# A two-block network in one launch: in its linear-attention layer the weights' low parts move to VectorE, the state is carried to the middle of the next block, the head norm's weights are applied after the transposition, and pools start elsewhere

## The chip, the cores and the metric

The kernel runs on one core of one Trainium2 chip, in one launch. The metric is the device time of one execution in microseconds. Before the change the median of three timed runs is 2821.83 us (2821.72 to 2823.71). Nothing is batched: 512 tokens of width 1024 go through the whole network once, and everything is computed in float32 accuracy.

## The reference, cut to what matters

The network is a chain of nine stages: an "even" layer (recurrence), an "odd" layer (gated linear attention), a feed-forward, a stick-breaking attention, two feed-forwards with shared keys and values between them, a sparse attention and a last feed-forward. The change touches the odd layer; of it, per head (4 heads, keys 128 wide, values 256 wide) and per direction (forward and backward):

```
z = lr @ w_gate + b_gate;  g = log_sigmoid(z) / 16
bcum = cumsum(g in a block);  btot = its last
q_in = q * exp(bcum);  k_in = k * exp(-bcum);  k_st = k * exp(btot - bcum)
o_intra = (mask * (q_in @ k_in.T)) @ v
o_inter = q_in @ state;   state = exp(btot) * state + k_st.T @ v
o = rmsnorm(o_f + o_b, head_norm_g);   y = (o * silu(r)) @ w_out
x = x + rmsnorm(y, norm_post)
```

The kernel uses blocks of 128 tokens, so there are four blocks and, per head and direction, three state updates.

## The kernel before, in words

Every product in full accuracy is three matmuls. A float32 operand is split into a high part, rounded to the chip's fast float32 format, and a low part, the rest; `mm3` (lines 88 to 92) issues high x high, high x low and low x high into one PSUM tile. So each 128x2048 slab of weights that arrives by DMA (`wload`, lines 75 to 86, tile `ws`) costs two ScalarE copies of 128x1024 (`wh`, line 84) and two subtractions of 128x1024 (`wl`, line 85). The subtraction is on VectorE, or on GpSimd where the caller passes `eng=nc.gpsimd`. There are two buffers each of `ws`, `wh` and `wl`; SyncE issues all DMAs, and the next slab's DMA waits until the subtraction has read `ws`.

The odd layer (`odd`, lines 601 to 864) starts with `begin` (query and key products of heads 0 and 1 while the stage before still finishes), and then runs a loop of 48 steps, 12 for each head, written in lines 832 to 859. The loop calls, step by step: `scaled` and `scores` (query and key scaled by the decay, block products `A`, transposed keys `KT`), `state` (line 685: the product `U` of keys and values of a block, the new state `S`, and its split into `Sh`, high and low), `decay` of the next head (line 627: the gate's logarithm, a scan over 512 tokens, exponentials), `outputs` (line 730: products into PSUM tile `o`, squares for the norm, statistics `st`), and at a head's end `gated` (line 752: `o` times norm times gate, transposed by TensorE into `ot`, split into `oh` and `ol`). Between them the list `dense` hands out the dense products of other heads: `queries`, `values`, `gate` and `out`, with a due step for each piece. In the whole layer 13 slabs (heads 1 to 3 of values, heads 2 and 3 of queries, all gates, three output slabs, and the first slab of the feed-forward behind) have their low part on GpSimd. A scheduler then sets each engine's order from these calls; each engine runs its instructions in that fixed order and waits on semaphores.

In `decay`, the minimum of line 636 is on VectorE and the subtraction of line 637 on GpSimd. In `state`, `S` is carried as of the block's end: line 697 multiplies it by the block's decay, line 698 adds `U` times a factor, and lines 702 and 703 multiply by the factor to the next block's middle and split. In `gate`, line 722 (VectorE) scales, line 725 (ScalarE) applies silu, and line 727 (GpSimd) multiplies by the head norm's weights `og`. Line 681 (GpSimd) adds the two directions' masked products.

Tiles are placed on two stacks of pools. The pool `sb` lives for the whole kernel and holds the weights' buffers, the activations `xh` and `xl`, and at its end a tile `rtok` of 32 columns (128 bytes in each partition). A stage's own pool starts right behind it. In the built program, the tiles of `ffn0`, `ffn1`, `ffn3`, the odd layer and the stick-breaking stage start at addresses that leave a remainder of 224 when divided by 256 (the first `uh` of `ffn0`: byte 125152); the weights, the activations, and all tiles of `ffn2` (whose pool starts behind another stage's, at byte 156000) leave 96. In a feed-forward (lines 1502 to 1555), `pj` is the first product (activations move through the array) and `y` the second (`uh` and `ul` move through it).

Of the kernel before, what the change touches and what calls it, by code (L numbers as in the profile page):

```python
# [17 lines left out]
EPS = 1e-6  # L18
# [20 lines left out]
_CC = [("ident", 128), ("one", 2), ("eps", 2), ("half", 2)]  # L39
# [5 lines left out]
def _room(n):  # L45

    return -(-n // 32) * 32
# [19 lines left out]
class Kernel:  # L67
# [231 lines left out]
    def run(self):  # L299
        tc, nc, A = self.tc, self.nc, self.A  # L300
        with ExitStack() as stack:
# [4 lines left out]
                                 "rtok": 1, "xh": 1, "xl": 1})  # L306
# [3 lines left out]
            with tc.high_priority():  # L310
# [7 lines left out]
                nc.sync.dma_start(cc, A["cc"])  # L318
# [34 lines left out]
    def even(self):  # L353
# [11 lines left out]
        with tc.tile_pool(name="ev", bufs=1, reuse_waits="tile") as p0, tc.tile_pool(name="evp", bufs=1, space=PSUM, reuse_waits="tile") as pp:  # L365
# [10 lines left out]
            hb = p0.tile([128, 32], F32, name="hb")  # L376
# [224 lines left out]
    def odd(self):  # L601
        tc, nc, A, prm = self.tc, self.nc, self.A, self.prm
        x, N = self.xn, self.N
        with tc.tile_pool(name="od", bufs=1, reuse_waits="tile") as p0, \
# [22 lines left out]
            def decay(h, d):  # L627
# [8 lines left out]
                nc.vector.tensor_scalar(z, ps, b, 0.0, op0=OP.add, op1=OP.min)  # L636
                nc.gpsimd.tensor_tensor(u, z, u, OP.subtract)
# [3 lines left out]
                sm = p.tile([128, 3, 4], F32, tag="sm", name="sm")  # L641
                zb = blocks(z)
                nc.vector.tensor_tensor(blocks(u), zb, zb[:, :, mid:mid + 1].to_broadcast([128, 4, 128]), OP.subtract)
                nc.scalar.activation(sm[:, 0, :], zb[:, :, mid], AF.Exp, scale=1.0 / 16)
# [18 lines left out]
            def scores(h, d):  # L663
# [16 lines left out]
                if d:  # L680
                    nc.gpsimd.tensor_tensor(t, H["A"][0], t, OP.add)
# [3 lines left out]
            def state(h, d, a):  # L685
# [13 lines left out]
                H["S"][d] = Sn  # L699
                f = sm[:, 0, n:n + 1]  # L700
                Sh, Sl = (p.tile([128, 256], F32R, tag="Sh", name="Sh") for _ in range(2))
                nc.scalar.activation(Sh, Sn, AF.Copy, scale=f)
                nc.vector.scalar_tensor_tensor(Sl, Sn, f, Sh.bitcast(F32), op0=OP.mult, op1=OP.subtract)
# [13 lines left out]
            def gate(h):  # L717
                w = self.wload(A["od_r"][h], eng=nc.gpsimd)
                gr = heads[h]["gr"] = p.tile([128, 4, 256], F32, tag="gr", name="gr")
                for j in range(4):  # L720
                    ps = self.proj_t(w, x, j)
                    nc.vector.tensor_scalar(gr[:, j, :], ps, rt[:, j:j + 1], None, op0=OP.mult)
# [4 lines left out]
                nc.gpsimd.tensor_tensor(gr, gr, og[:, None, :].to_broadcast([128, 4, 256]), OP.mult)  # L727
# [24 lines left out]
            def gated(h):  # L752
# [61 lines left out]
            og = self.bcast(p0, A["od_g"], 256, "og")  # L814
# [17 lines left out]
            for t in range(49):  # L832
# [848 lines left out]
```

## Time and profile before

| | |
|---|---|
| median of three runs | 2821.83 us |
| the profiled execution's own time | 2823.5 us |
| its span, first to last instruction | 2821.8 us |
| TensorE (PE) busy | 2730.9 us, 97% |
| VectorE (DVE) busy | 1711.3 us, 61% |
| ScalarE (ACT) busy | 1215.5 us, 43% |
| GpSimd (POOL) busy | 495.6 us, 18% |
| mean granted TensorE clock | 0.987 of full speed |

The profile is of one execution. Each engine has busy time; TensorE's matmuls overlap (a matmul of 512 columns is listed with 389 ns, and the next one starts before it ends), so their durations add up to more than the busy time. An engine's wait is put down to the instruction that released it. The granted clock is 1.0 (2.4 GHz) or 0.5 (1.2 GHz) at any one time; a mean in between says how the time is shared. In the line numbers, 85 and 84 are those of `wload`, 95 and 96 those of the split helper `hilo`, and 90 to 92 those of `mm3`, whoever calls them; the tile's name tells the caller.

### The profile page before, as it was taken

Reading aid. Unit: us, or ns where it says so; the run is one execution under the profiler, and the core shown is the slowest. Engines: PE = TensorE matmul, PEld = TensorE weight load, DVE = VectorE, ACT = ScalarE, POOL = GpSimd, SP = SyncE. Lnnn points to the kernel's source line nnn. Section 1 sums busy time; section 2 is a strip of 40 time slices with the busy share of each in tenths; the row PEclk is TensorE's granted clock in tenths of the full one; section 3 lists DMA queues with packets and bytes.
Section 4 is the critical chain, followed back from the end, with each engine's and each line's share of the span. In section 5 each row is a group of like instructions: output and inputs, shape, how many; then the busy total and the mean of one; then the engine's idle time right before and its main releaser. Section 6 shows DMA issues by size and latency. Waiting matters only on the chain.

```text
span 2821.8 us, 35042 instructions
## 1 busy us (share of the span) xinstructions
PE 2730.9 (97%) x13879; PEld 2303.0 (82%) x13879; DVE 1711.3 (61%) x2656; ACT 1215.5 (43%) x2044; POOL 495.6 (18%) x493
## 2 busy tenths in 40 slices
PE   9999989988999999999999999999999899999999
PEld 7788878887888887888788888988888787888887
DVE  8877878667443357888533346744346887643433
ACT  6533446544322236777422233432233676532221
POOL 1434334333000012111100002100001445300000
PEclk9999999999999999999999999999999999999999
DMA  4232241212223232111223224532224111022322
GB/s 150 92 99 101 85 147 65 79 49 83 90 89 106 94 104 76 46 60 61 75 83 99 102 81 138 172 105 86 101 89 141 53 46 57 31 90 97 107 84 86
DMA packets 51557, 253.62 MB, mean 90 GB/s; under 512 B 6336, under 2 KB 11712, under 8 KB 29760
## 3 DMA queue, kind: packets, MB, share of 16 engines
q1 hardware_dynamic: 51392, 251.37, 26.4%
q8 instruction: 109, 1.79, 0.3%
q14 instruction: 56, 0.46, 0.1%
HBM read 241.91 MB, written 8.39 MB: 89 GB/s over the span
## 4 chain that ended last, share of the span: by engine, by line
PE 71%; DVE 8%; ACT 3%; issue 1%; POOL 1%; DMA 0%; SPq 0%; DVEq 0%; ACTq 0%; POOLq 0%
PE pj L90 12%; PE pj L91 12%; PE pj L92 12%; PE y L90 7%; PE y L91 7%; PE y L92 7%; PE pjt L90 2%; PE pjt L92 2%; PE pjt L91 2%; PE z L920 1%; DVE wl L85 1%; PE o L1416 1%; ACT wh L84 1%; PE pt L1398 1%; ACT P L1383 1%
## 5 line engine op out<-in xcount | busy, mean ns | idle before, releaser
L90 PE MATMUL pj<-xh,wh 128*128 128x512 f32 (+1 forms) x2112 | 808.5, 384 | 17.3 <-ACT xh L183 10.7
L91 PE MATMUL pj<-xl,wh 128*128 128x512 f32 (+1 forms) x2112 | 808.1, 383 | 3.2 <-DVE xl L184 3.0
L92 PE MATMUL pj<-xh,wl 128*128 128x512 f32 (+1 forms) x2112 | 805.2, 382 | 0.7 <-DVE wl L85 0.6
L84 ACT ACTIVATE wh<-ws 128x1024 fp32r<-128x1024 f32 x464 | 431.9, 978 | 764.5 <-PE y L91 317.5
L90 PEld LDWEIGHTS pj<-xh,wh 128*128 128x128 f32 x2112 | 399.2, 190 | 96.9 <-ACT xh L183 12.7
L91 PEld LDWEIGHTS pj<-xl,wh 128*128 128x128 f32 x2112 | 400.8, 190 | 83.0 <-DVE xl L184 6.8
L85 DVE TENSOR_TENSOR wl<-ws,wh 128x1024 fp32r<-128x1024 f32 (+2 forms) x400 | 434.7, 1127 | 51.6 <-ACT wh L84 50.7
L92 PEld LDWEIGHTS pj<-xh,wl 128*128 128x128 f32 x2112 | 400.8, 190 | 77.6 <-DVE wl L85 1.3
L92 PE MATMUL y<-uh,wl 128*128 128x512 f32 x704 | 277.0, 394 | 0.0
L90 PE MATMUL y<-uh,wh 128*128 128x512 f32 x704 | 277.0, 393 | 0.0
L91 PE MATMUL y<-ul,wh 128*128 128x512 f32 x704 | 277.0, 393 | 0.0
L141 POOL TENSOR_TENSOR acc<-acc,sq 128x256 f32<-128x256 f32 (+1 forms) x70 | 74.3, 1061 | 1150.3 <-ACT sq L140 1150.3
L1534 DVE TENSOR_TENSOR u<-pj,s 128x512 f32<-128x512 f32 x88 | 60.8, 691 | 292.6 <-PE pj L92 287.9
L1549 DVE SCALAR_TENSOR_TENSOR yt<-y,R 128x512 f32<-128x512 f32 x64 | 44.3, 692 | 257.5 <-PE y L92 257.5
L90 PE MATMUL pjt<-wh,xh 128*128 128x256 f32 x640 | 185.9, 290 | 5.4 <-DVE v L954 1.9
L92 PE MATMUL pjt<-wh,xl 128*128 128x256 f32 x640 | 183.3, 286 | 0.0
L91 PE MATMUL pjt<-wl,xh 128*128 128x256 f32 x640 | 183.0, 286 | 0.0
L85 POOL TENSOR_TENSOR wl<-ws,wh 128x1024 fp32r<-128x1024 f32 x64 | 163.7, 2577 | 103.3 <-ACT wh L84 93.9
L1530 DVE TENSOR_TENSOR a<-pj,R 128x512 f32<-128x512 f32 x88 | 60.8, 691 | 190.3 <-PE pj L92 190.2
L92 PEld LDWEIGHTS y<-uh,wl 128*128 128x128 f32 x704 | 132.2, 188 | 30.9
L91 PEld LDWEIGHTS y<-ul,wh 128*128 128x128 f32 x704 | 132.2, 188 | 30.9
L90 PEld LDWEIGHTS y<-uh,wh 128*128 128x128 f32 x704 | 132.2, 188 | 30.9
(415 smaller groups left out, 4308.6 us busy)
## 6 DMA issues: line engine op xcount, KB each, us to landing
ws<-in_ffn_in SPq DMA_DIRECT2D x88, 1024.0 KB, 4.8
ws<-in_ffn_out SPq DMA_DIRECT2D x32, 768.0 KB, 4.3
ws<-in_ev_in SPq DMA_DIRECT2D x23, 1024.0 KB, 4.8
ws<-in_ffn_out SPq DMA_DIRECT2D x32, 640.0 KB, 3.9
ws<-in_ev_out SPq DMA_DIRECT2D x8, 1024.0 KB, 4.8
ws<-in_sb_qk SPq DMA_DIRECT2D x8, 1024.0 KB, 4.8
ws<-in_kv_w SPq DMA_DIRECT2D x6, 1024.0 KB, 4.9
ws<-in_od_qk SPq DMA_DIRECT2D x4, 1024.0 KB, 4.8
```

The costliest lines, as they stand in the source:

```text
L84: nc.scalar.activation(wh[:, a:b], ws[:, a:b], AF.Copy)
L85: (eng or nc.vector).tensor_tensor(wl[:, a:b], ws[:, a:b], wh[:, a:b].bitcast(F32), OP.subtract)
L90: mm(ps, L[0], R[0], start=start, stop=False)
L91: mm(ps, L[0], R[1], start=False, stop=False)
L92: mm(ps, L[1], R[0], start=False, stop=stop)
L141: self.acc.tensor_tensor(N["acc"][:, s], N["acc"][:, s], q[:, s], OP.add)
L920: nc.tensor.matmul(z[:, c + w - w2:c + w], tri if k2 == kb else neg, H["L"][i][t][:, c2:c2 + w2], start=False, stop=True, skip_group_check ...
L1383: nc.scalar.activation(P[:, a], P[:, a], AF.Exp, bias=c1[:, n:n + 1], scale=-1.0, accum_out=c1[:, 2 + n:3 + n])
L1398: nc.tensor.transpose(pt[:, r, :], Ps[u][r][:, n * nk + 128 * kb:n * nk + 128 * kb + 128], self.ident)
L1530: nc.vector.tensor_tensor(a, a_, N["R"], OP.mult)
L1534: nc.vector.tensor_tensor(u, b_, s, OP.mult)
L1549: nc.vector.scalar_tensor_tensor(t, ps, 0.5, N["R"], op0=OP.mult, op1=OP.mult)
```

## The change

In `odd`: all weights' low parts that were on GpSimd go to VectorE, and so do the additions of lines 637 and 681. The minimum of line 636 becomes part of the addition's instruction, and the bias is added by a ScalarE copy. The state is kept as of the next block's middle: the factor between two middles is formed once per head and direction in a product of three columns; the first state is two ScalarE copies from PSUM, later ones are one VectorE instruction. The gate's scaling goes to ScalarE. The head norm's weights are no longer multiplied into the gate, but are the per-partition factor where `ot` is split; `og` becomes two columns. Elsewhere: `rtok` moves into the table `cc`, which has 136 columns instead of 134, small tiles are rounded to 64 columns, and two buffer counts of the sparse attention shrink, which moves the pools. After it, `uh` of `ffn0` starts at byte 125024 (remainder 96), and all feed-forward, odd and stick-breaking tiles leave 96; in the sparse attention the tiles `P`, `ch` and `vm` go from 96 to 32.

```
-_CC = [("ident", 128), ("one", 2), ("eps", 2), ("half", 2)]
+_CC = [("ident", 128), ("one", 4), ("rtok", 4)]
-    return -(-n // 32) * 32
+    return -(-n // 64) * 64
-        r = self.sb.tile([128, 32], F32, tag="rtok", name="rtok")[:, :4]
+        r = self.cc["rtok"]
...
-                nc.vector.tensor_scalar(z, ps, b, 0.0, op0=OP.add, op1=OP.min)
-                nc.gpsimd.tensor_tensor(u, z, u, OP.subtract)
+                nc.scalar.activation(z, ps, AF.Identity, bias=b)
+                nc.vector.scalar_tensor_tensor(u, z, 0.0, u, op0=OP.min, op1=OP.subtract)
...
-                nc.scalar.activation(sm[:, 1, :], zb[:, :, end], AF.Exp, scale=1.0 / 16)
-                nc.vector.tensor_copy(sm[:, 2, :], zb[:, :, end])
+                a, n = (0, 1) if d == 0 else (1, 0)
+                nc.vector.tensor_tensor(sm[:, 4 + a:7 + a], zb[:, a:a + 3, end], sm[:, n:n + 3], OP.mult)
...
-                    nc.gpsimd.tensor_tensor(t, H["A"][0], t, OP.add)
+                    nc.vector.tensor_tensor(t, H["A"][0], t, OP.add)
...
+                r = [sm[:, 4 + i:5 + i] for i in order]
+                if a:
+                    X = p.tile([128, 256], F32, tag="S", name="S")
+                    if a == 1:
+                        nc.vector.tensor_tensor(X, U, H["S"][d], OP.add)
+                    else:
+                        nc.vector.scalar_tensor_tensor(X, H["S"][d], r[1], U, op0=OP.mult, op1=OP.add)
+                    U = X
+                nc.scalar.activation(Sh, U, AF.Copy, scale=r[a])
                 if a == 0:
-                    nc.vector.tensor_scalar(Sn, ps, sm[:, 2, j:j + 1], None, op0=OP.mult)
-                else:
-                    nc.vector.tensor_scalar(Sn, H["S"][d], sm[:, 1, j:j + 1], None, op0=OP.mult)
-                    nc.vector.scalar_tensor_tensor(Sn, ps, sm[:, 2, j:j + 1], Sn, op0=OP.mult, op1=OP.add)
+                    X = p.tile([128, 256], F32, tag="S", name="S")
+                    nc.scalar.activation(X, U, AF.Copy, scale=r[0])
+                nc.vector.scalar_tensor_tensor(Sl, U, r[a], Sh.bitcast(F32), op0=OP.mult, op1=OP.subtract)
...
-                w = self.wload(A["od_v"][h], eng=nc.gpsimd if h else None)
+                w = self.wload(A["od_v"][h])
-                w = self.wload(A["od_r"][h], eng=nc.gpsimd)
+                w = self.wload(A["od_r"][h])
-                    nc.vector.tensor_scalar(gr[:, j, :], ps, rt[:, j:j + 1], None, op0=OP.mult)
+                    nc.scalar.activation(gr[:, j, :], ps, AF.Copy, scale=rt[:, j:j + 1])
-                nc.gpsimd.tensor_tensor(gr, gr, og[:, None, :].to_broadcast([128, 4, 256]), OP.mult)
...
-                    self.hilo(pt[e], oh, ol)
+                    nc.scalar.activation(oh, pt[e], AF.Copy, scale=og[:, e:e + 1])
+                    nc.vector.scalar_tensor_tensor(ol, pt[e], og[:, e:e + 1], oh.bitcast(F32), op0=OP.mult, op1=OP.subtract)
...
-                wh, wl = self.wload(A["od_out"][h], eng=nc.gpsimd)
+                wh, wl = self.wload(A["od_out"][h])
-            og = self.bcast(p0, A["od_g"], 256, "og")
+            og = p0.tile([128, 64], F32, name="og")
+            nc.sync.dma_start(og[:, :2], A["od_g"])
-                    self.w0 = self.wload(A["ffn_in0"][0], eng=nc.gpsimd)
+                    self.w0 = self.wload(A["ffn_in0"][0])
...
-                                    "vm": 1, "c": 2, "c1": 12, "c16": 1, "b": 1, "sq": 1, "oh": 1, "ol": 1})
+                                    "vm": 1, "c": 2, "c1": 10, "c16": 1, "b": 1, "sq": 1, "oh": 1, "ol": 1})
```

The scheduler makes new orders of it, from the odd layer's loop to its end; the other stages keep theirs. On VectorE, at the end of head 0 (`gk`, `gq`: the split of head 1's scaled keys and queries; `st`: head 0's norm; `o`: the gated output that TensorE transposes), the order before is:

```order
L780 TENSOR_TENSOR qk<-pj,R 128x512
L655 TENSOR_TENSOR tmp<-qk,tmp 128x512
L96 TENSOR_TENSOR gq<-tmp,gq 128x512
L96 TENSOR_TENSOR gk<-tmp,gk 128x512
L748 TENSOR_SCALAR st<-st 128x4
L96 TENSOR_TENSOR gq<-tmp,gq 128x512
L161 TENSOR_TENSOR st<-st 128x4
L162 TENSOR_TENSOR st<-st 128x4
L163 TENSOR_SCALAR st<-st 128x4
L713 SCALAR_TENSOR_TENSOR vl<-pjt,rtok,vh 128x256
L750 TENSOR_TENSOR st<-st 128x4
L758 SCALAR_TENSOR_TENSOR o<-o,st,gr 128x256 x4
```

In the same place of the changed kernel (its lines 655, 656, 718, 752, 754 and 762 answer to 654, 655, 713, 748, 750 and 758), the order is:

```order
L785 TENSOR_TENSOR qk<-pj,R 128x512
L96 TENSOR_TENSOR gk<-tmp,gk 128x512
L85 TENSOR_TENSOR wl<-ws,wh 128x1024 x2
L96 TENSOR_TENSOR gq<-tmp,gq 128x512
L752 TENSOR_SCALAR st<-st 128x4
L96 TENSOR_TENSOR gq<-tmp,gq 128x512
L161 TENSOR_TENSOR st<-st 128x4
L162 TENSOR_TENSOR st<-st 128x4
L718 SCALAR_TENSOR_TENSOR vl<-pjt,cc,vh 128x256
L163 TENSOR_SCALAR st<-st 128x4
L754 TENSOR_TENSOR st<-st 128x4
L762 SCALAR_TENSOR_TENSOR o<-o,st,gr 128x256 x4
```

A pair of `wl` subtractions now stands ahead of the two `gq` splits and so of the norm and the gated outputs; the rest is as it was.

On VectorE, in the loop's third head, where `out(1)` adds its products to the residual tiles (`h_61` to `h_68`) between the state updates (`S`, `Sh`) and the decay of head 3 (`tmp<-cg,tmp` is the scan), the order before is:

```order
L639 SCALAR_TENSOR_TENSOR tmp<-cg,tmp 128x512
L722 TENSOR_SCALAR gr<-pjt,rtok 128x256
L648 COPY sm<-tmp 128x4
L643 TENSOR_TENSOR tmp<-tmp 128x512
L655 TENSOR_TENSOR tmp<-qk,tmp 128x512
L795 TENSOR_TENSOR h_63<-y,h_63 128x512
L698 SCALAR_TENSOR_TENSOR S<-U,sm,S 128x256
L654 TENSOR_TENSOR tmp<-qk,tmp 128x512
L697 TENSOR_SCALAR S<-S,sm 128x256
L795 TENSOR_TENSOR h_64<-y,h_64 128x512
L795 TENSOR_TENSOR h_65<-y,h_65 128x512
L698 SCALAR_TENSOR_TENSOR S<-U,sm,S 128x256
```

After the change the same stretch, a little longer, is:

```order
L85 TENSOR_TENSOR wl<-ws,wh 128x1024 x2
L800 TENSOR_TENSOR h_63<-y,h_63 128x512
L698 TENSOR_TENSOR S<-U,S 128x256
L800 TENSOR_TENSOR h_64<-y,h_64 128x512
L800 TENSOR_TENSOR h_65<-y,h_65 128x512
L700 SCALAR_TENSOR_TENSOR S<-S,sm,U 128x256
L800 TENSOR_TENSOR h_66<-y,h_66 128x512
L637 SCALAR_TENSOR_TENSOR tmp<-tmp 128x512
L708 SCALAR_TENSOR_TENSOR Sh<-S,sm,Sh 128x256
L639 SCALAR_TENSOR_TENSOR tmp<-cg,tmp 128x512
L800 TENSOR_TENSOR h_67<-y,h_67 128x512
L85 TENSOR_TENSOR wl<-ws,wh 128x1024 x2
```

The gate's scaling and the state's multiplication by the decay are gone from it, the additions to `h` stand closer together, and two pairs of `wl` subtractions stand among them.

On VectorE at the end of head 3, the last in the loop, the order before is:

```order
L795 TENSOR_TENSOR h_66<-y,h_66 128x512
L750 TENSOR_TENSOR st<-st 128x4
L758 SCALAR_TENSOR_TENSOR o<-o,st,gr 128x256 x2
L795 TENSOR_TENSOR h_67<-y,h_67 128x512
L795 TENSOR_TENSOR h_68<-y,h_68 128x512
L758 SCALAR_TENSOR_TENSOR o<-o,st,gr 128x256 x2
L96 TENSOR_TENSOR ol<-ot,oh 128x512 x2
```

After the change it is:

```order
L754 TENSOR_TENSOR st<-st 128x4
L762 SCALAR_TENSOR_TENSOR o<-o,st,gr 128x256
L800 TENSOR_TENSOR h_67<-y,h_67 128x512
L762 SCALAR_TENSOR_TENSOR o<-o,st,gr 128x256
L800 TENSOR_TENSOR h_68<-y,h_68 128x512
L762 SCALAR_TENSOR_TENSOR o<-o,st,gr 128x256
L85 TENSOR_TENSOR wl<-ws,wh 128x1024 x2
L762 SCALAR_TENSOR_TENSOR o<-o,st,gr 128x256
L769 SCALAR_TENSOR_TENSOR ol<-ot,og,oh 128x512 x2
```

The pair for the first slab of the feed-forward behind, which was GpSimd's, stands between the third and the fourth gated output.

## Rows read from the trace of the kernel before

**Rows 1.** The page: span, busy time of the engines.

```profile
span 2821.8 us, 35042 instructions
...
PE 2730.9 (97%) x13879; PEld 2303.0 (82%) x13879; DVE 1711.3 (61%) x2656; ACT 1215.5 (43%) x2044; POOL 495.6 (18%) x493
```

**Rows 2.** Windows: ffn0, ffn2, odd loop: length; PE, PEld, DVE, ACT, POOL busy; clock.

```profile
720.00:1060.00 340.00, 339.92 (x1484) 278.22 (x1484) 149.20 (x176) 99.72 (x132) 8.61 (x7) 1.00 0.29 97
...
1800.00:2170.00 370.00, 369.43 (x1664) 305.73 (x1663) 172.25 (x219) 120.28 (x166) 7.94 (x7) 1.00 0.32 107
...
430.00:660.00 230.00, 208.78 (x1406) 189.85 (x1405) 163.82 (x254) 121.02 (x222) 87.16 (x40) 0.96 0.19 66
```

**Rows 3.** Feed-forwards ffn0, ffn2: groups of TensorE: count, busy us, mean ns.

```profile
L91 PE MATMUL pj<-xl,wh 128*128 128x512 f32 x314 | 122.2, 389 | 0.0
...
L90 PE MATMUL y<-uh,wh 128*128 128x512 f32 x167 | 66.0, 395 | 0.0
...
L90 PE MATMUL y<-uh,wh 128*128 128x512 f32 x174 | 67.7, 389 | 0.0
```

**Rows 4.** Windows of 60 us within `y`, ffn0 and ffn2: PE busy (matmuls).

```profile
826.00:886.00 60.00, 60.00 (x259) 48.27 (x258) 4.84 (x7) 0.00 (x0) 1.00 0.30 101
...
1940.00:2000.00 60.00, 60.00 (x266) 49.73 (x265) 4.84 (x7) 0.00 (x0) 1.00 0.31 101
```

**Rows 5.** Waits of TensorE in the odd loop: total us, times, longest.

```profile
PE ot L760 <- DVE o L758: 7.9, 4, 3.3
PE y L90 <- DVE h L795: 4.1, 1, 4.1
PE o L91 <- DVE Sh L703: 2.1, 2, 1.9
PE y L92 <- POOL wl L85: 1.8, 1, 1.8
PE y L90 <- DVE gr L722: 1.5, 1, 1.5
```

**Rows 6.** VectorE in order of time, before three of these waits: start, duration.

```profile
489.62 2.89 DVE L655 TENSOR_TENSOR tmp<-qk,tmp 128x512 f32<-128x512 f32 x1
492.43 2.89 DVE L96 TENSOR_TENSOR gq<-tmp,gq 128x512 fp32r<-128x512 f32 x1
...
594.24 2.83 DVE L655 TENSOR_TENSOR tmp<-qk,tmp 128x512 f32<-128x512 f32 x1
...
611.67 2.26 DVE L162 TENSOR_TENSOR st<-st 128x4 f32<-128x4 f32 x1
```

**Rows 7.** Two lines of VectorE: duration ns minimum/median/maximum.

```profile
L655 DVE TENSOR_TENSOR tmp<-qk,tmp x8: 682/692/2890, 449.7 to 603.3; 128x512 f32<-128x512 f32 x8
...
L697 DVE TENSOR_SCALAR S<-S,sm x16: 342/354/2384, 467.5 to 645.1; 128x256 f32<-128x256 f32 x16
```

**Rows 8.** Groups of GpSimd in the odd loop: count, busy us, mean ns.

```profile
L85 POOL TENSOR_TENSOR wl<-ws,wh 128x1024 fp32r<-128x1024 f32 x24 | 60.8, 2553 | 55.7 <-ACT wh L84 46.3 <-issue 8.1 <-POOL tmp L637 1.3
```

**Rows 9.** Groups of VectorE: `wl` in ffn0, then three of the odd loop.

```profile
L85 DVE TENSOR_TENSOR wl<-ws,wh 128x1024 fp32r<-128x1024 f32 x52 | 62.0, 1221 | 3.7 <-ACT wh L84 3.6
...
L697 DVE TENSOR_SCALAR S<-S,sm 128x256 f32<-128x256 f32 x16 | 14.9, 931 | 0.3
...
L722 DVE TENSOR_SCALAR gr<-pjt,rtok 128x256 f32<-128x256 f32 x16 | 7.6, 478 | 9.1 <-PE pjt L92 9.1
...
L695 DVE TENSOR_SCALAR S<-U,sm 128x256 f32<-128x256 f32 x8 | 3.8, 478 | 0.9 <-PE U L92 0.7
```

**Rows 10.** ScalarE in the odd loop: copies from PSUM, 512 and 256 columns.

```profile
L712 ACT ACTIVATE vh<-pjt,rtok 128x256 fp32r<-128x256 f32 x16 | 7.4, 465 | 15.4 <-PE pjt L92 13.6 <-DVE rtok L172 1.8
...
L633 ACT ACTIVATE tmp<-z,prm 128x512 f32<-128x512 f32 x8 | 5.5, 684 | 2.5 <-PE z L630 2.5
```

**Rows 11.** Window at half clock, the first of five in the loop.

```profile
477.80:481.10 3.30, 3.30 (x11) 2.73 (x11) 3.30 (x5) 2.35 (x5) 1.23 (x2) 0.50 0.02 5
```

More of the change, by code (lines that the diff above doesn't have):

```diff
@@ L305, in run @@
             self.sb = Bufs(sb0, {"ws": 2, "wh": 2, "wl": 2, "sq": 1, "acc": 2, "R": 1,
-                                 "rtok": 1, "xh": 1, "xl": 1})
+                                 "xh": 1, "xl": 1})
             cc = sb0.tile([128, _offsets(_CC)[1]], F32, name="cc")
@@ L317, in run @@
                         nc.sync.dma_start(self.prm, A["prm"])
-                nc.sync.dma_start(cc, A["cc"])
+                nc.sync.dma_start(cc[:, :132], A["cc"])
             self.cc = Table(cc, _CC)
@@ L375, in even @@
             e, d, v, v2, q, c2, c4 = (sm[:, j, :] for j in range(7))
-            hb = p0.tile([128, 32], F32, name="hb")
+            hb = p0.tile([128, 64], F32, name="hb")[:, :32]
             def constants():
@@ L640, in decay @@
                 mid, end = (63, 127) if d == 0 else (64, 0)
-                sm = p.tile([128, 3, 4], F32, tag="sm", name="sm")
+                sm = p.tile([128, 16], F32, tag="sm", name="sm")
                 zb = blocks(z)
                 nc.vector.tensor_tensor(blocks(u), zb, zb[:, :, mid:mid + 1].to_broadcast([128, 4, 128]), OP.subtract)
-                nc.scalar.activation(sm[:, 0, :], zb[:, :, mid], AF.Exp, scale=1.0 / 16)
-                nc.scalar.activation(sm[:, 1, :], zb[:, :, end], AF.Exp, scale=1.0 / 16)
+                nc.scalar.activation(sm[:, 0:4], zb[:, :, mid], AF.Exp, scale=1.0 / 16)
                 nc.scalar.activation(z, u, AF.Exp, scale=1.0 / 16)
                 nc.scalar.activation(u, u, AF.Exp, scale=-1.0 / 16)
-                nc.vector.tensor_copy(sm[:, 2, :], zb[:, :, end])
+                a, n = (0, 1) if d == 0 else (1, 0)
+                nc.vector.tensor_tensor(sm[:, 4 + a:7 + a], zb[:, a:a + 3, end], sm[:, n:n + 3], OP.mult)
                 return z, u, sm
@@ L690, in state @@
                 j, n = order[a], order[a + 1]
-                ps = ps_.tile([128, 256], F32, tag="c", name="U")
-                self.mm3(ps, (KT[0][:, j, :], KT[1][:, j, :]), H["V"][j], True, True)
-                Sn = p.tile([128, 256], F32, tag="S", name="S")
-                if a == 0:
-                    nc.vector.tensor_scalar(Sn, ps, sm[:, 2, j:j + 1], None, op0=OP.mult)
-                else:
-                    nc.vector.tensor_scalar(Sn, H["S"][d], sm[:, 1, j:j + 1], None, op0=OP.mult)
-                    nc.vector.scalar_tensor_tensor(Sn, ps, sm[:, 2, j:j + 1], Sn, op0=OP.mult, op1=OP.add)
[L699 to L703, printed above, removed]
+                U = ps_.tile([128, 256], F32, tag="c", name="U")
+                self.mm3(U, (KT[0][:, j, :], KT[1][:, j, :]), H["V"][j], True, True)
+                r = [sm[:, 4 + i:5 + i] for i in order]
[6 more added lines that the diff above has]
+                    U = X
+                Sh, Sl = (p.tile([128, 256], F32R, tag="Sh", name="Sh") for _ in range(2))
+                nc.scalar.activation(Sh, U, AF.Copy, scale=r[a])
+                if a == 0:
+                    X = p.tile([128, 256], F32, tag="S", name="S")
+                    nc.scalar.activation(X, U, AF.Copy, scale=r[0])
+                H["S"][d] = X
+                nc.vector.scalar_tensor_tensor(Sl, U, r[a], Sh.bitcast(F32), op0=OP.mult, op1=OP.subtract)
                 H["Ss"][d][n] = (Sh, Sl)
             def values(h):
-                w = self.wload(A["od_v"][h], eng=nc.gpsimd if h else None)
+                w = self.wload(A["od_v"][h])
                 for j in range(4):
@@ L769, in queries @@
                 if ps is None:
-                    w, ps = self.wload(A["od_qk"][h], eng=nc.gpsimd), []
+                    w, ps = self.wload(A["od_qk"][h]), []
                     for m in range(2):
@@ L1341, in compressed @@
                 nc.vector.tensor_tensor(p4, pt.rearrange("p j (r n) -> p j r n", r=4), msk, OP.add)
-                c1 = p.tile([128, 4, 16], F32, tag="c16", name="c16")
+                c1 = p.tile([128, 3, 16], F32, tag="c16", name="c16")
                 mx, l, f = (c1[:, i, :] for i in range(3))
@@ L1590, in _constants @@
     p = np.arange(128)
-    one = np.ones((128, 2), np.float32)
-    cc = np.concatenate([np.eye(128), one, EPS * one, 0.5 * one], 1)
+    one = np.ones((128, 4), np.float32)
+    cc = np.concatenate([np.eye(128), one], 1)
     low = (p[:, None] <= p[None, :])
@@ L1634, in arrays @@
     o["od_lr"] = np.concatenate([_cols(w[:, 3072:], 32)[0], g.reshape(128, 1024)], 1)
-    o["od_g"] = I["gla_norm_g"]
+    o["od_g"] = _feat(I["gla_norm_g"])
     w = I["odd_w_out"][0]
```

## The prediction, made before the changed kernel had run

> **What bounds the kernel now.** I read the page first: TensorE is busy for 97% of the span [rows 1], so little but its idle time, its clock and the pace of its matmuls can be won. Then the windows by stage: in the feed-forwards TensorE idles for 0.1 us of 340, but in the odd layer's loop it works for 208.8 of 230 us at a mean clock of 0.96 [rows 2]. So the loop has 21.2 us of waiting; and as the clock is either whole or half, a mean of 0.96 over 230 us means 18 us at half clock, which do the work of 9, a loss of 9.2 us. The list of TensorE's waits says who is late there: nearly always VectorE, with the gated outputs `o` (7.9 us in four waits), an addition to the residual (4.1), a state's low part (2.1), the gate's scaling (1.5), and once GpSimd with a low part (1.8) [rows 5]. The half clock comes in five stretches of some 3.4 us that begin in such a wait or within a microsecond behind it; the first is shown [rows 11].
>
> Why VectorE is late shows in the order of time: a multiplication of 128x512 took 2.89 us, then a subtraction of the same size 2.89, elsewhere an operation on four columns 2.26 [rows 6], while the same line's median is 0.692 us and the state's multiplication has a median of 0.354 and a maximum of 2.384 [rows 7]. GpSimd is busy for 87 us of the 230 [rows 2], mostly with `wl` at 2.553 us each [rows 8]; VectorE's excess is about one such instruction's length. So I read it as VectorE being held while GpSimd reads SBUF.
>
> The third thing is the matmuls' pace. In `ffn0` a `pj` matmul is listed with 389 ns and a `y` matmul with 395; in `ffn2` `y` has 389 as well [rows 3]. Counted, 60 us of `y` hold 259 matmuls in `ffn0` and 266 in `ffn2`, TensorE busy throughout at full clock [rows 4]. The code is the same; of what I can see only the place of `uh` and `ul` differs: remainder 224 in `ffn0`, 96 in `ffn2`.
>
> **The change part by part.**
>
> *Pools.* `ffn0`, `ffn1` and `ffn3` take the placement of `ffn2`. Each has 8 outputs of 12 and of 10 slices with 3 matmuls, 528; three stages have 1584. At 60/259 - 60/266 us = 6.1 ns each [rows 4] this is 9.7 us, all on the path, since TensorE never idles there. Other moved matmuls of 512 columns (about 290 in the stick-breaking stage, 150 in the odd layer) could give 0 to 440 x 6.1 ns = 2.7 us; they stand among shorter ones and waits, so I take 1. The sparse attention's move to remainder 32 is shown by no row; its some 450 matmuls of 128 columns could cost or give 6 ns each, 2.7 us either way; I take 0. Together -10.7.
>
> The Trainium skill speaks against this: "SBUF — State Buffer", section "Who interferes with whom", has TensorE wait for no other reader, and knows no address that slows it. By that rule the term would be 0; the trace disagrees, with 395 against 389 ns, and I go by the rows [rows 3, 4].
>
> *Low parts.* 13 slabs, 26 subtractions, go from GpSimd to VectorE at 1.221 us [rows 9]: 31.7 us. The added sum of the two directions is four times 0.69 us [rows 7], 2.8 us. VectorE loses the state's multiplication (5.7 us at its median [rows 7]), the first state's scaling (3.8) and the gate's (7.6) [rows 9], 17.1 in all; the minimum and the added product of three columns replace instructions of the same kind. Against this, GpSimd has nothing left in the loop, so that the holds go: 16 x (0.931 - 0.354) = 9.2 us in the state's multiplication alone [rows 7, 9], 8.6 us in the four instructions shown [rows 6], and with the like ones I put them at 25 to 36 us. VectorE's 164 us [rows 2] become 164 + 34.5 - 17.1 less these, some 150. ScalarE gets 16 gate copies and 8 state copies at 0.465 us and 8 bias copies at 0.684 [rows 10], and loses 8 small exponentials: +15 us on 121 [rows 2], with room. GpSimd's hop in the decay chain goes; the scan now waits for VectorE itself. On SyncE a slab's DMA waits for the subtraction that frees `ws`, which now takes 2.4 us a pair where GpSimd took 5.1; so slabs come earlier, and no DMA moves past another that TensorE waits for. The head norm's weights ride on instructions that were there; their multiplication on GpSimd, which `o` waited for in the last two heads, is gone.
>
> What TensorE still waits for, wait by wait [rows 5]. The addition's 4.1, the state's 2.1, GpSimd's 1.8 and the gate's 1.5 have their cause removed: 9.5 us. Of the four `o` waits the longest, 3.3 us at head 2's end, had more than 2 us of hold in the norm, and 1.0 stays. Of the other 4.6 most is head 0's, with 2 x 2.2 us of holds ahead; but the new order puts a pair of 2.44 us ahead of `gq`, so 0.9 stays of it, and 1.7 at the other two heads. New: the pair before head 3's last `o`, behind which nothing is left for TensorE but `y` itself, 2.4 us; and two pairs in `out(1)` with one in `out(2)`, where TensorE has two PSUM tiles and 1.4 us of matmuls to each addition, together 2.0. Such a pair also waits for ScalarE's copy and the DMA, with the splits, the norm and `o` queued behind it, and TensorE behind them; the row shows 3.7 us of that for 52 subtractions [rows 9], so I add nothing. Left: 1.0 + 0.9 + 1.7 + 2.4 + 2.0, and 3.8 of small waits that I leave as they are, 11.8 of 21.2 us; gain 9.4. Of the five half-clock stretches I keep two: 9.2 x 3/5 = 5.5 us gained. The loop: -14.9. Its bounds are -30.4, all of it, and +28 (below).
>
> The Trainium skill's "Perfetto Trace Analysis", section "Optimizing Scalar/DVE Operations", would offload a saturated VectorE to GpSimd, the reverse of this edit. Here VectorE is busy for 71% and its late instructions are the held ones; by that rule the loop would lose.
>
> *Sum.* -9.7 - 1.0 - 14.9 = -25.6. The profiled execution took 2823.5 us, 1.7 above the median of the three runs: 2798 for one like it, and 2821.8 - 25.6 = 2796 as median.
>
> **The rivals.**
>
> A. *Exchange.* The new pairs in VectorE's queue cost what the holds did; the pools' gain stays: 2821.8 - 10.7 = 2811. For it: VectorE's order is fixed, 13 pairs of 2.44 us are 32 us, as much as the 25 to 36 that go. Against it: a hold falls wherever GpSimd happens to run, while a pair's place is chosen by the scheduler; of the 13 I find four ahead of something that TensorE soon waits for.
>
> B. *The address isn't it.* The `y` matmuls stay at 395 ns, and the loop alone gains: 2821.8 - 14.9 = 2807. The rule of the Trainium skill's "SBUF — State Buffer" cited above speaks for it. Against it, three stages show 395 and the one with the other placement 389 [rows 3].
>
> C. *All goes.* No wait of the loop is left and the clock stays whole, pools at their upper bound: 2821.8 - 30.4 - 12.4 = 2779. Against it: the waits at the heads' ends come from a chain (squares, norm, `o`, transposition), not from holds alone.
>
> D. *Slower: VectorE's queue becomes the bound of the loop.* Each of 13 pairs stands whole between TensorE and its next operand, 31.7 us, and each brings a half-clock stretch at 9.2/5 = 1.8 us, 24 us; less the 28 that go is +28, less 10.7 gives 2839. It turns slower from 41 us of new loss on, which is ten of the thirteen pairs. Against it: VectorE idles for 66 of 230 us now.
>
> **How the numbers follow.** The forecast has 0.55 (2790 to 2802 by itself), A 0.20, B 0.08, C 0.08, D 0.04; 0.05 lies between A and D, with some new loss that eats most of the pools' gain. I call no change what lies within 0.2%, 5.6 us, about what a measurement of this kernel can tell. Faster takes the forecast, A, B and C: 0.91; same 0.05; slower 0.04. For 8 in 10 the range has to reach past A above and nearly to C below: 2783 to 2812.
>
> **What would show it.** Pools: `y` in all feed-forwards at 389 ns, 266 matmuls in 60 us. Holds: the maxima of the scaling lines near 0.7 us, GpSimd idle from 430 us to the loop's end. The loop's end earlier by some 15 us, with a mean clock near 0.98. Wrong, if TensorE waits for `wl` on VectorE or for `o` behind it by more than 15 us in the loop, or if `y` stays at 395 ns.

## The result, and the profile after

The changed kernel takes 2789.33 us (median of four runs, 2788.91 to 2790.28) against 2821.77 of the kernel before, run beside it; the ratio is 0.9885, with a 95% interval of 0.987 to 0.990. It is faster by 32.4 us; 2796 was forecast, in a range of 2783 to 2812. The forecast by itself was given 2790 to 2802, and the time lies 0.7 us below that.

The page of the kernel after, to be held against [rows 1]:

```profile
span 2788.6 us, 34998 instructions
...
PE 2711.2 (97%) x13879; PEld 2297.2 (82%) x13879; DVE 1692.1 (61%) x2646; ACT 1227.3 (44%) x2068; POOL 403.6 (14%) x451
```

The span is shorter by 33.2 us. Where they went can be read from the starts of the same matmuls in the two traces, since only the odd layer has a new order:

| from the start of ... | before, us | after, us | difference |
|---|---|---|---|
| the kernel to the dense part of ffn0 (odd layer) | 710.6 | 689.9 | -20.8 |
| ffn0 | 345.7 | 342.1 | -3.5 |
| stick-breaking stage | 311.7 | 310.7 | -0.9 |
| ffn1 | 351.9 | 348.4 | -3.5 |
| keys and values, ffn2 | 446.8 | 446.7 | -0.1 |
| sparse attention | 285.5 | 284.4 | -1.1 |
| ffn3 | 364.6 | 361.0 | -3.5 |
| the end | 5.1 | 5.4 | +0.3 |

The windows of the kernel after (columns as in [rows 2], behind the clock the DMA's share and GB/s): the odd layer's loop to the last transposition, the stretch from there to ffn0's first product, called the tail below, and 60 us of `y` in ffn0.

```profile
428.00:638.60 210.60, 204.68 (x1423) 187.48 (x1421) 146.53 (x248) 133.69 (x248) 0.00 (x0) 0.99 0.21 73
638.60:663.10 24.50, 17.88 (x107) 16.35 (x107) 15.88 (x32) 11.98 (x28) 9.48 (x12) 0.78 0.18 60
...
804.00:864.00 60.00, 60.00 (x266) 49.72 (x265) 24.75 (x32) 13.37 (x17) 0.00 (x0) 1.00 0.31 107
```

The loop and the tail of the kernel before:

```profile
428.00:661.50 233.50, 211.62 (x1422) 191.80 (x1420) 165.59 (x258) 122.88 (x224) 88.19 (x41) 0.96 0.19 66
661.50:684.00 22.50, 15.53 (x107) 13.99 (x107) 15.79 (x32) 11.84 (x28) 13.22 (x15) 0.97 0.20 65
```

GpSimd does nothing in the loop, where it was busy for 87 us [rows 2], and 60 us of `y` now hold 266 matmuls in ffn0 too, where [rows 4] have 259. The duration listed for `y` there, 395 ns in [rows 3], is the other stage's 389:

```profile
L90 PE MATMUL y<-uh,wh 128*128 128x512 f32 x176 | 68.5, 389 | 0.0
```

TensorE's waits in the loop, against [rows 5]:

```profile
PE ot L764 <- DVE o L762: 3.0, 3, 2.2
PE pjt L90 <- DVE vl L718: 1.8, 1, 1.8
PE y L90 <- ACT h L798: 0.5, 1, 0.5
PE pjt L90 <- ACT gr L727: 0.2, 1, 0.2
PE pjt L90 <- DVE h L800: 0.2, 1, 0.2
```

The gated outputs `o` are waited for at the last head, but for 0.2 us at the second; VectorE's additions to `h`, 4.1 us in one wait before, cost 0.2. The line with the maximum of 2890 ns in [rows 7] (line 656 after) now has the same duration every time:

```profile
L656 DVE TENSOR_TENSOR tmp<-qk,tmp x8: 684/686/693, 449.5 to 591.6; 128x512 f32<-128x512 f32 x8
```

One wait is new and was foreseen: the pair of `wl` for the slab of ffn0 that stands before head 3's last `o`. VectorE, then TensorE, in order of time (start, duration; in brackets the idle time before and what ended it):

```profile
635.35 2.35 DVE L85 TENSOR_TENSOR wl<-ws,wh 128x1024 fp32r<-128x1024 f32 x2
637.62 0.48 DVE L762 SCALAR_TENSOR_TENSOR o<-o,st,gr 128x256 f32<-128x256 f32 x1
```

```profile
638.15 0.44 PE L764 MATMUL ot<-cc,o 128*128 128x128 f32 x2 [2.22 <-DVE o L762]
```

Behind this wait TensorE runs at half clock, 1.2 GHz, which [rows 11] show for the loop of before:

```profile
638.90:645.40 6.50, 6.06 (x25) 5.47 (x26) 2.69 (x5) 2.13 (x5) 0.74 (x1) 0.50 0.35 146
```

The trace's record of the granted clock has 17.1 us at half in the loop before and 3.4 after, but in the tail 1.3 before and 10.7 after. Of these 10.7 us, 6.8 are the stretch behind the wait. The other 3.9 begin a second stretch of 6.8 us (659.2 to 666.1), which the kernel before has as well (682.6 to 689.4); in these 3.9 us TensorE has nothing to do, since it waits 5.8 us there for ScalarE's `sq`, in both kernels. The loop got 22.9 us shorter (233.5 to 210.6) and the tail 2.1 us longer (22.4 to 24.5).

### The profile page after: what moved, and what is told of

It reads as the page before. It is cut to its first block, busy times and chain, and to the rows that moved or that the text cites. A ratio compares the mean times of both kernels' runs of the same rounds, so it can differ in the third digit from the quotient of the medians.

```text
span 2788.6 us, 34998 instructions
## 1 busy us (share of the span) xinstructions
PE 2711.2 (97%) x13879; PEld 2297.2 (82%) x13879; DVE 1692.1 (61%) x2646; ACT 1227.3 (44%) x2068; POOL 403.6 (14%) x451
## 4 chain that ended last, share of the span: by engine, by line
PE 79%; DVE 11%; ACT 4%; POOL 2%; issue 2%; DMA 1%; SPq 0%; DVEq 0%; POOLq 0%; ACTq 0%
PE pj L90 14%; PE pj L91 14%; PE pj L92 14%; PE y L90 7%; PE y L92 7%; PE y L91 7%; PE pjt L90 2%; PE pjt L92 2%; PE pjt L91 2%; DVE wl L85 2%; PE z L926 1%; ACT wh L84 1%; PE o L1422 1%; POOL wl L85 1%; PE pt L1404 1%
## 5 line engine op out<-in xcount | busy, mean ns | idle before, releaser
L85 DVE TENSOR_TENSOR wl<-ws,wh 128x1024 fp32r<-128x1024 f32 (+2 forms) x426 | 465.1, 1133 | 59.3 <-ACT wh L84 58.5
L90 PEld LDWEIGHTS pj<-xh,wh 128*128 128x128 f32 x2112 | 397.9, 189 | 97.8 <-ACT xh L183 13.7
L95 ACT ACTIVATE uh<-u 128x512 fp32r<-128x512 f32 x88 | 54.9, 624 | 173.6 <-DVE u L1540 173.4
```

The source lines that it names most:

```text
L85: (eng or nc.vector).tensor_tensor(wl[:, a:b], ws[:, a:b], wh[:, a:b].bitcast(F32), OP.subtract)
L90: mm(ps, L[0], R[0], start=start, stop=False)
L95: self.nc.scalar.activation(hi, src, AF.Copy)
```

## The experiments

Twelve kernels were run. The table has nine of them beside before and after; the three on addresses come last. For each: median of its runs, and from the profile of one execution the loop's length, TensorE's idle time and time at half clock in it, busy time of VectorE and GpSimd, all in us, and the holds, that is what VectorE's instructions take beyond the median of their line and shape (where over 0.15 us; of two middle ones the shorter is taken, and the sums are good to some 0.3 us). L is the low parts on VectorE, S the state, G the gate's scaling and the norm's weights, D the decay's subtraction and the sum of the directions; all but the first have the new placement. TensorE's order in the loop is the same in before and pools_only, and in after and w0_pool. In all others the scheduler made a new one, so what a part gives there includes what its order gives or takes; the two were not separated.

| kernel | parts | median us | loop | PE idle | half | DVE | POOL | holds |
|---|---|---|---|---|---|---|---|---|
| before | none | 2821.8 | 233.5 | 21.9 | 17.1 | 165.6 | 88.2 | 36.4 |
| pools_only | none | 2809.6 | 233.9 | 22.0 | 17.1 | 165.7 | 88.2 | 36.4 |
| state_only | S | 2803.8 | 227.0 | 16.9 | 13.7 | 144.0 | 86.7 | 21.8 |
| gate_only | G | 2809.2 | 229.4 | 22.4 | 10.2 | 154.3 | 78.3 | 30.9 |
| decay_only | D | 2807.7 | 230.9 | 20.7 | 17.1 | 164.9 | 72.7 | 32.9 |
| low_only | L | 2802.9 | 225.5 | 16.6 | 15.2 | 164.8 | 28.2 | 6.3 |
| state_low | S L | 2801.1 | 223.3 | 16.0 | 10.2 | 157.8 | 26.5 | 6.8 |
| rest_only | S G D | 2795.1 | 216.9 | 12.0 | 3.4 | 139.2 | 62.6 | 21.0 |
| no_state | G D L | 2790.4 | 211.4 | 6.6 | 3.7 | 154.9 | 0.0 | 0.0 |
| after | all | 2789.3 | 210.6 | 5.9 | 3.4 | 146.5 | 0.0 | 0.0 |
| w0_pool | all, one slab less | 2785.3 | 207.4 | 4.0 | 0.0 | 144.2 | 1.1 | 0.0 |

**pools_only.** The kernel before with the edits to `rtok`, `cc`, `_room`, `hb`, `c1` and `c16` alone.

> The kernel before with the change's placement of the pools alone (every tile at the address it has after the change; the odd layer's code as before). Theory 'address': the y products of ffn0, ffn1 and ffn3 take 226.7 ns from start to start in place of 233.3, 1584 x 6.65 ns = 10.5 us, the stick-breaking stage gives 0.9, the sparse attention 1.1, the odd layer at most 1: 2808 us (2807 to 2811). Rival 'not the address', the feed-forwards' gain follows from the odd layer's new order: no change, 2821.8.

2809.61 us (2807.75 to 2812.40; ratio 0.9955, interval 0.9943 to 0.9968): 12.5 us, as the theory of the address has it; the odd layer's loop is as long as before. The table of stages gives the same sum, 10.5 in the three feed-forwards, 0.9 and 1.1. How much of the last two is the address is not shown: in pools_only's profile they are 1.9 each, and the time at half clock in the sparse attention is 23.9 us before, 20.5 in pools_only and 13.7 after.

**low_only.** pools_only with

```
-                w = self.wload(A["od_r"][h], eng=nc.gpsimd)
+                w = self.wload(A["od_r"][h])
```

and so for all 13 slabs.

> Placement as after, and of the odd layer's edits one alone: the 13 slabs' low parts on VectorE. State, gate, norm and decay as before. Theory 'holds': what kept VectorE late is GpSimd's reading of SBUF; with it gone most of the odd layer's 20.9 us comes by this edit alone, 15 to 20 us: 2789 to 2793. Rival 'VectorE's load': moving 31.7 us of subtractions to VectorE pays only because the other edits take 17 us off it; alone it gives less than half, 0 to 9 us: 2799 to 2808.

2802.88 us (2802.20 to 2803.24): 6.7 us, so the theory of the holds misses by 10, although the holds are down from 36.4 to 6.3 us, and the rival, VectorE's load, fits. TensorE's longest waits in this loop:

```profile
PE y L90 <- DVE h L795: 5.2, 1, 5.2
PE ot L760 <- DVE o L758: 3.1, 3, 2.2
PE o L90 <- ACT Sh L702: 2.5, 1, 2.5
PE A L90 <- ACT gq L95: 2.4, 1, 2.4
```

The first of them in VectorE's order of time, and what GpSimd does meanwhile:

```profile
583.70 1.23 DVE L639 TENSOR_TENSOR_SCAN tmp<-cg,tmp 128x512 f32<-128x512 f32 x1 [0.66 <-POOL tmp L637]
584.84 0.67 DVE L96 TENSOR_TENSOR gk<-tmp,gk 128x512 fp32r<-128x512 f32 x1
585.42 2.36 DVE L85 TENSOR_TENSOR wl<-ws,wh 128x1024 fp32r<-128x1024 f32 x2
587.69 2.83 DVE L643 TENSOR_TENSOR tmp<-tmp 128x512 f32<-128x512 f32 x1
590.44 0.68 DVE L795 TENSOR_TENSOR h<-y,h 128x512 f32<-128x512 f32 x1
```

```profile
587.07 2.90 POOL L727 TENSOR_TENSOR gr<-gr,og 128x1024 f32<-128x1024 f32 x1 [3.41 <-ACT gr L725]
```

A pair of `wl` and one of the few holds left, beside the multiplication by `og`, stand one behind the other ahead of the addition, with an idle stretch of the scan for GpSimd ahead of both.

**rest_only.** The changed kernel with `eng=nc.gpsimd` at the 13 slabs again.

> The changed kernel with one part undone: the 13 slabs' low parts are on GpSimd again. State, gate, norm, decay and placement as after. Theory 'holds': GpSimd's 60 us of reading stay, so do the holds, and most of the loop's gain goes: 2800 to 2807, with VectorE operations of over 2 us in the loop again. Rival 'VectorE's load': the other edits carry the gain, 2789 to 2796.

2795.14 us (2792.88 to 2802.67). Holds are there as expected (line 656 has a maximum of 2821 ns again, 21.0 us in all), but 14.5 of the 20.3 us came without moving the low parts, by a median with a wide scatter (two of five runs took 2801 and 2803). The rival, VectorE's load, fits again; at this point the holds looked like the wrong cause.

**state_only, gate_only, decay_only.** pools_only with the diff's hunks of one part each: `decay`'s factors with `state`; `gr`, `og` and the split of `ot`; lines 636, 637 and 681.

> pools_only (2809.6) with one more edit: the state carried as of the next block's middle. Low parts, gate, norm and decay as before. The three parts state, gate with norm, and decay together gave 14.5 us (pools_only 2809.6, rest_only 2795.1). Theory 'VectorE's time': the gain goes by the time an edit takes off VectorE, holds included; the state's multiplication was 14.9 us with its holds, the first scaling 3.8, so some 60% of the three: 2801 (2799 to 2803). Rival 'heads' ends': what counts is the chain to the gated output, which the state isn't on: 2807 or more.

> pools_only (2809.6) with one more edit: the gate's scaling on ScalarE, the head norm's weights on the split outputs and not on GpSimd. Low parts, state and decay as before. Theory 'VectorE's time': it takes off 7.6 us of scaling and 8.8 us of holds that lie beside the multiplication by og: 2804 (2802 to 2806). Rival 'heads' ends': o waits no more for the multiplication by og, the heads' waits of 7.9 us and their half clock go: 2799 or less.

> pools_only (2809.6) with one more edit: the decay's subtraction and the sum of the two directions on VectorE, the bias on ScalarE. Theory 'VectorE's time': it adds 2.8 us to VectorE and takes off 3.0 us of holds, nothing is won: 2809.6 (2808 to 2811). Rival 'hop': the chain from gate to scan, which crosses VectorE, GpSimd and VectorE, gets shorter, and the scaled keys come earlier: 2805 or less.

2803.76 us (2801.94 to 2805.14), 2809.18 (2805.55 to 2812.48) and 2807.71 (2806.11 to 2808.16). The state alone gives 5.9 us, the gate 0.4 within a scatter of 7, the decay 1.9. The runs of the last two overlap with those of pools_only, so that the state's gain alone is clear of the scatter. The theory of VectorE's time was near for the state and wrong for the gate, the heads' ends wrong for both, and the decay's 1.9 lies between its two. (gate_only's profile is of an execution 3.6 us below its median.) In gate_only the one long wait of before has merely grown:

```profile
PE ot L759 <- DVE o L757: 7.7, 4, 2.9
PE y L90 <- DVE h L795: 6.5, 1, 6.5
```

Together the three give 14.5, not 8.2.

**no_state** undoes S alone in the changed kernel; **state_low** puts S on low_only.

> The changed kernel with one part undone: the state is carried as before. So GpSimd has nothing to do in the odd layer's loop, as after the change, while VectorE keeps the state's multiplications (some 9.5 us more than after it). Theory 'holds': they were what TensorE waited for; with all of them gone the time is near the changed kernel's, 2789 to 2793. Rival 'VectorE's queue': what counts is all that stands in VectorE's queue ahead of an operand, work and holds alike; 9.5 us more of work bring TensorE's waits for the residual's addition and for Sh back, 2795 to 2801.

> pools_only (2809.6) with two edits: the state as after and the low parts on VectorE; gate, norm and decay as before, on GpSimd. Alone the state gave 5.9, the low parts 6.7. Theory 'additive': 2797. Rival 'stacking' (a pair of subtractions and a hold stand ahead of one operand, and its wait goes only when both are gone): the state's edit also takes off 3.8 of the 6.3 us of holds that low_only has left, so more than the sum: 2791 to 2795.

no_state takes 2790.43 us (2789.41 to 2791.29): the holds' forecast, and not the queue's, though VectorE has 8.4 us more to do than after the change. Its longest waits:

```profile
PE pjt L90 <- DVE vl L713: 1.8, 1, 1.8
PE ot L759 <- DVE o L757: 0.8, 2, 0.6
PE y L90 <- ACT h L793: 0.5, 1, 0.5
```

state_low takes 2801.07 (2799.27 to 2802.23), less gain than the sum of its two parts, so neither theory fits it; the wait for `h` is there, 4.6 us, with the same pair and the same held instruction ahead of it. So the loop doesn't follow VectorE's busy time (144.0 us in state_only, loop 227.0; 154.9 in no_state, loop 211.4), and not the holds alone (6.3 us in low_only, loop 225.5; 21.0 in rest_only, 216.9). It is shortest where GpSimd is out of it, and GpSimd can cost in two ways: as a reader that holds VectorE, and as a hop in the chains. The list of VectorE's waits in the loop of before has the scan waiting for GpSimd's subtraction, 6.5 us in five waits:

```profile
DVE tmp L639 <- POOL tmp L637: 6.5, 5, 2.0
```

From low_only to no_state, that is by G and D, it is 12.5 us; how they share these was not run.

The trace of before shows the same within one order. TensorE waits 15 times in the loop for more than 0.15 us, 21.4 us in all. Eight of these waits, 14.8 us, are for the end of a run of VectorE's instructions, without a gap of over 0.15 us, that has held ones in it (one through a copy of ScalarE's). One, 1.8 us, is for GpSimd's own `wl`, and two, 2.1 us, are for runs that began late because of GpSimd's subtraction. The other four, 2.7 us, have nothing of GpSimd ahead of them. In rest_only 6.9 of the 12.0 us are of the first two kinds, and after the change none.

**w0_pool.** The changed kernel with one slab back:

```
-                    self.w0 = self.wload(A["ffn_in0"][0])
+                    self.w0 = self.wload(A["ffn_in0"][0], eng=nc.gpsimd)
```

> The changed kernel with one slab's low part on GpSimd again, the first slab of the feed-forward behind, whose pair of subtractions stands between the third and the fourth gated output of the last head. Theory 'this pair costs': TensorE's wait of 2.2 us for the last o goes, and with it the 6.8 us at half clock that begin in it, 3.4: 2784 (2782 to 2786), below both kernels. Rival 'hold': GpSimd holds VectorE there for as long as the pair took, or TensorE falls to half clock in the tail anyway: 2787 to 2790.

2785.28 us (2784.57 to 2785.64; ratio 0.9870, interval 0.9856 to 0.9883), the fastest of all, 4.0 us below the changed kernel by the medians (not run side by side; before beside them had 2821.75 and 2821.77). The wait of 2.2 us is gone from the loop, and the tail is 1.0 us shorter than the changed kernel's:

```profile
636.10:659.60 23.50, 16.66 (x106) 15.11 (x106) 15.85 (x32) 11.91 (x28) 13.08 (x14) 0.90 0.19 62
```

At its start TensorE still runs at half clock, for 3.4 us in place of 6.8, so the rival's fall of the clock in the tail is there in part. Another 1.0 us lies ahead of the first head's transposition and is not shown to be the slab's: both profiles have the same order and the same wait of 1.8 us for `vl` there, but behind it the changed kernel's has 3.4 us at half clock and w0_pool's none. GpSimd works through the last outputs, and nothing of VectorE is held:

```profile
634.98 4.70 POOL L85 TENSOR_TENSOR wl<-ws,wh 128x1024 fp32r<-128x1024 f32 x2 [209.46 <-ACT wh L84]
```

```profile
634.69 0.87 DVE L762 SCALAR_TENSOR_TENSOR o<-o,st,gr 128x256 f32<-128x256 f32 x2
636.70 1.41 DVE L769 SCALAR_TENSOR_TENSOR ol<-ot,og,oh 128x512 fp32r<-128x512 f32 x2 [1.14 <-ACT oh L768]
```

Both lines read one operand from PSUM. Such lines are not held in the loop before either: the 16 additions to `h` from PSUM, five of them beside a GpSimd instruction, have no long one,

```profile
L795 DVE TENSOR_TENSOR h<-y,h x16: 677/684/692, 584.2 to 659.5; 128x512 f32<-128x512 f32 x16
```

while all 23 held instructions lie beside a GpSimd instruction. Over all lines, 33 VectorE instructions that read PSUM start while GpSimd works, and none is held; of 26 that read SBUF alone, 23 are.

**sweep_a, sweep_b, shift_all.** The changed kernel with a pad ahead of each feed-forward's tiles (here sweep_a's, in bytes; in ffn3 of sweep_b, `uh` and `ul` are 128 bytes longer instead), in shift_all with one of 128 bytes ahead of `ws`, so that everything moves together.

```
+            pad = (32, 64, 96, 160)[f]
+            if pad:
+                p0.tile([128, pad // 4], F32, name="pad")
```

> The changed kernel with a pad ahead of each feed-forward's tiles, so that uh and ul start at remainder 128 (ffn0), 160 (ffn1), 192 (ffn2), 0 (ffn3) of 256, the weights at 96 as before. Theory 'upper half': a moving operand that starts in the upper half of 256 bytes costs 6.65 ns: y at 233.3 ns from start to start in ffn0, ffn1, ffn2 (528 each, 10.5 us in all, 2800) and 226.7 or less in ffn3. Rival 'distance': only a distance of 128 from the weights' remainder costs: 226.7 in all four, 2789.

> The changed kernel with uh and ul at remainder 32 (ffn0), 64 (ffn1) and 224 (ffn2), and in ffn3 the slices in turn at 96 and 224; the weights at 96. sweep_a gave 233.3 ns at 128, 228.9 at 160, 233.4 at 192, 234.3 at 0, where 96 gives 226.7. Theory 'only an equal remainder is free': 32 and 64 cost as well, 229 to 234 ns, 224 in ffn2 gives 233.3, and in ffn3 only half of the matmuls cost, mean 230. Rival 'what counts is 96 itself or its neighbours': 64 stays at 226.7.

> The changed kernel with 128 bytes ahead of the weights' buffers, so that weights, activations, uh and ul and all stages' tiles start at remainder 224 in place of 96, the distances between them unchanged. Theory 'distance': it is the remainder against that of the weights that counts: y and pj at 226.7 ns, 2789 us. Rival 'address': a moving operand at 224 costs 6.65 ns wherever the weights are: pj (6336 matmuls, most of 512 columns) and y (2112) go to 233.3, some 50 us more, 2830 to 2845.

60 us of `y` in each feed-forward of sweep_a (remainders 128, 160, 192, 0), then of sweep_b (32, 64, 224, and 96 and 224 in turn):

```profile
804.00:864.00 60.00, 60.00 (x259) 48.21 (x258) 23.11 (x30) 12.64 (x17) 0.00 (x0) 1.00 0.30 103
1466.00:1526.00 60.00, 60.00 (x264) 49.24 (x263) 24.34 (x31) 12.42 (x16) 0.00 (x0) 1.00 0.30 101
1914.00:1974.00 60.00, 60.00 (x259) 48.27 (x258) 23.22 (x30) 12.38 (x16) 0.00 (x0) 1.00 0.31 101
2562.00:2622.00 60.00, 60.00 (x258) 48.24 (x257) 23.01 (x30) 12.38 (x16) 0.00 (x0) 1.00 0.30 101
```

```profile
804.00:864.00 60.00, 60.00 (x258) 48.06 (x258) 23.12 (x31) 12.76 (x17) 0.00 (x0) 1.00 0.31 102
1467.00:1527.00 60.00, 60.00 (x259) 48.31 (x258) 23.20 (x30) 12.57 (x17) 0.00 (x0) 1.00 0.30 102
1918.00:1978.00 60.00, 60.00 (x259) 48.27 (x258) 23.24 (x31) 11.84 (x15) 0.00 (x0) 1.00 0.30 101
2566.00:2626.00 60.00, 60.00 (x262) 48.80 (x261) 23.96 (x31) 12.07 (x16) 0.00 (x0) 1.00 0.30 101
```

258 or 259 matmuls at every remainder but 160 (264) and the weights' own 96 (266 or 267 elsewhere); with half of the slices at 96, 262. Neither theory of sweep_a holds: neither the upper half nor a distance of 128 alone is the rule. The theory of sweep_b that only an equal remainder is free holds at all of them. In shift_all `y` and then `pj`, with everything at 224:

```profile
804.00:864.00 60.00, 60.00 (x267) 49.67 (x266) 24.48 (x31) 12.19 (x16) 0.00 (x0) 1.00 0.30 101
872.00:932.00 60.00, 60.00 (x267) 49.67 (x266) 22.69 (x26) 16.43 (x21) 0.00 (x0) 1.00 0.26 88
```

224 costs nothing when the weights are at 224 as well, as the theory of the distance has it. The times, one run each, are 2800.06, 2801.60 and 2788.26 us.

## Why the prediction was right, and where its sizes were off

**Pools: right, a little small.** 9.7 us stood in the sum for the three feed-forwards and 10.5 came: 60 us hold whole matmuls only, and from start to start it is 233.3 ns before and 226.7 after, 6.65 ns and not 6.1. The other moved matmuls had 1.0; their stages gave 2.1, in which the half clock has an unknown part. What I took for the place of `uh` and `ul` is their distance from the weights' place, by sweep_b and shift_all; the change brings both to 96. The rule of the Trainium skill's "SBUF — State Buffer", section "Who interferes with whom", that TensorE never waits for anyone, does not cover this: TensorE needs 226.7 ns with equal remainders and 233 to 234 with nearly all others, with the same work beside it. So rival B falls.

**Holds: right as a mechanism, wrong in what removes them.** 25 to 36 us were foreseen to go, and 36.4 went; every one of the 23 lay beside GpSimd. The Trainium skill's "SBUF — State Buffer", section "Who interferes with whom", also says that a VectorE instruction with two SBUF inputs contends with a GpSimd instruction that reads SBUF, and one with at most one, outside its faster modes, does not. Lines 655 (2890 ns at most) and 795 (692) agree; lines 697 and 648 have one and were held, 2384 and 1910 ns at most, so they would be in such a mode, which no row shows. But the prediction put all of this under the low parts and did not ask what they give without the other edits. They alone gave 6.7 of the loop's 20.3 us, because pairs took the holds' place (VectorE 165.7 us busy before them, 164.8 after), as rival A has it, and because GpSimd's multiplication and hops stayed. The hop was named in the prediction and priced at nothing; 6.5 us of VectorE's idle time hung on it, and 2.1 us of TensorE's waits follow it directly. That the total came near is in part luck: it needed the other edits as well, which the prediction did not price apart. The 17.1 us that VectorE loses were counted as well; by no_state the state's 9.5 of them are worth about 1 us, hardly more than the scatter, once GpSimd is out, and 5.9 while it is in.

**TensorE's waits: the step that was mis-sized.** 11.8 of 21.2 us were left in the list of waits; 5.9 of 21.9 stayed. The last pair was put at 2.4 and cost 2.2. The other `o` waits, put at 3.6 in all, cost 0.8, as there is no hold in the norm before them. (For the multiplication by `og`, which the prediction had `o` wait for, `o` does not wait in the trace of before; TensorE's transposition alone stands in its list, with 1.4 us.) The pairs in `out(1)` and `out(2)`, put at 2.0, cost 0.2 at most, the one wait for VectorE's `h`; and of the small waits taken as staying, those for ScalarE's `Sh` and for `lrs` went.

**The clock: right in the loop, wrong behind it.** Three of five half-clock stretches were to go, and in the loop the time at half in which TensorE works fell from 15.9 to 3.4 us; half of the difference, 6.2 us, is gained, against 5.5. But the prediction stopped at the loop's end, and behind the wait for the last `o` come 6.8 us at half clock in the tail. In the tail, TensorE works for 6.3 us at half clock where it did for 0.1: 3.1 us lost by the same account, and the tail is 2.1 us longer in all. w0_pool has no such wait and is 4.0 us faster, by 2.2 us of wait, 1.0 of tail and some 1 us that is not shown to be the slab's.

Taken together: 10.7 forecast and 12.5 found for the placement; 14.9 forecast and 20.8 found for the odd layer. From the loop's start to the dense part of ffn0, 15.7 of these are TensorE's idle time and 4.4 the clock (half of the change in the time that TensorE works at half clock); 0.7 was not assigned.

**Rivals.** D would have shown as waits behind each of the 13 pairs; one cost more than 2 us. (The 28 us that go in D's sum come from no row; with the 30.4 that the prediction has elsewhere D would be 2836.) C's 2779 asked for all waits to go; w0_pool, with no more than 4.0 us idle, takes 2785.3. The Trainium skill's "Perfetto Trace Analysis", section "Optimizing Scalar/DVE Operations", says of a saturated VectorE that offloading some work to GpSimd may make sense, and adds that the two share a port, so that it might not help; that is weaker than the prediction had it. For 13 slabs it costs 5.8 us here (rest_only against after, with rest_only's scatter). For the one slab whose time falls on instructions that read PSUM it gains 4.0, some 3 of them by the wait and the tail.

## What to carry to other kernels

Judge work on GpSimd by what VectorE does at that moment: beside VectorE instructions that read SBUF alone it held 23 of 26 here, beside such as read PSUM none of 33. Single edits of one queue, each with its own order, don't add up: here 0.4, 1.9, 5.9 and 6.7 us alone are 20.3 together, and one of them is worth 1 in the end; to value an edit, undo it in the final kernel as well. And follow a wait past the stretch that is being improved: behind a wait of 2.2 us the next stretch got 2.1 us longer, with the half clock in it.

## What the runs showed of the hardware that was not expected

A float32 matmul of 512 columns starts 226.7 ns after the one before it when its moving operand and its weights start at the same remainder of 256 bytes, and 228.9 ns when the moving operand is 64 bytes above (remainder 160 against 96). At the other six remainders that were run (0, 32, 64, 128, 192 and 224 against 96) it is 233.3 to 234.3 ns (from the starts of 288 matmuls each). Moving all tiles together by 128 bytes changes nothing. Only multiples of 32 bytes were tried, and only with this stride of weights; where the conflict lies was not shown.
